# One layer of a hybrid encoder trunk: x is transposed before its norm, and the reciprocal rms goes onto the projections' results

## Chip, cores and metric

The kernel runs on one core of a Trainium2 chip. The metric is the device time of one execution in microseconds (us); lower is better. Engines: PE (TensorE), DVE (VectorE), ACT (ScalarE), POOL (GpSimd), SP (SyncE, which only issues transfers here).

## What is computed

One layer on 512 tokens of width 1024, batch 1. The part of the reference that the change touches:

```python
h = rms_norm(x, norm_mix_gain[l])      # x * rsqrt(mean(x*x) + eps) * gain
proj = h @ w_in[l]                     # 1024 x 3328, split into head groups
sb_q, sb_k, sb_v, hg_q, hg_f, hg_i, hg_g, mem_q = jnp.split(proj, split_points, axis=-1)
```

The head groups then go into stick-breaking attention (8 heads), a gated linear recurrence (4 heads) and attention into 256 memory tokens (4 heads). Their results are concatenated, multiplied by `w_out` and added to x. A retrieval over 16384 single-neuron experts follows (queries, top-k over product keys, gated sum of the chosen experts) and is added too. The rms of a token is one number for its row of h, so it may be applied to x before the product or to the row of `proj` after it.

## The kernel before

Tokens lie in four blocks of 128 (`xs[0..3]`). Every fp32 matmul operand is split in two: a rounded high part (`hhi`, `whi`) and the rest (`hlo`, `wlo`). A product is three matmuls, high by high, high by low, low by high (`mm3`, L413). Each matmul wants the contracted dimension on the partitions, so h is needed transposed: `hhi` and `hlo` hold k = 0..7 slices of 128 features by 512 tokens.

`x_norm` (L564) is the opening. It takes the squares' sums of the four blocks (ACT for blocks 0 and 2, DVE for 1 and 3), gets the reciprocal rms for two blocks at a time (`rsqrt`, L344: logarithm and exponential on ACT, one correction step on DVE), scales x by it into `hn`, and transposes: for each k one PSUM bank `nt` gets four 128x128 transposes, one per block; ACT evicts it times the gain into `hhi`, DVE evicts it again minus `hhi` into `hlo`.

`WStream` (L371) brings the weights: pieces of 128x1024 fp32, two to a chunk of 256 columns. `split` (L388) rounds a piece into `whi` (on DVE for piece 0, on ACT for the others) and subtracts for `wlo` (on POOL for pieces 0 and 1, on DVE later).

`in_proj` (L594) calls `x_norm` and then goes through the chunks. For the recurrence's f and q and the attention's q and k it uses `proj_f` (L479: 24 matmuls of 512 tokens for half a chunk; the result has features on partitions and tokens along the free dimension). For the values, the gates and the memory queries it uses `proj_t` (L489: tokens on partitions, 256 features). ACT evicts most results, with a sigmoid or a plain copy; `forget_bound` (L441) makes the constants `lb`, `omlb` (its scratch tile is `gmx`).

The order of the work is not written out by hand. `Threads` (L209) runs generators (`in_proj`, the recurrence `hgrn`, `sbreak`, `memattn`, `outproj`, `query`, `topk`, `gather`, `dense` and others), and `Pace` (L116) keeps modelled clocks for each engine; the generator that could go on first by that model emits its next step. The emitted instructions run in that order on each engine's in-order queue. A step whose modelled cost or engine changes can so move the steps of others. Transfers are issued on SP's queue; in this program each issue from the ninth on waits for the one eight places before it. Nearly all instructions bear L202, the helper that emits them, so the names of their tiles tell them apart.

Names in the rows: `nt` PSUM of transposes, `pf` and `pt` PSUM of `proj_f` and `proj_t`, `fkq` the recurrence's f, k, q, `hs` its scores, `hk`/`hkt` and `st`/`Sst` its transposed keys and state, `sz`, `se`, `sa`, `so` the attention's steps, `op` the output projection.

Of the kernel before, what the change touches and what calls it, by code (L numbers as in the profile page):

```python
# [7 lines left out]
F32 = mybir.dt.float32  # L8
# [6 lines left out]
AF = mybir.ActivationFunctionType  # L15
OP = mybir.AluOpType
# [4 lines left out]
P = 128  # L21
D = 1024
KD = 8
T = 512
NT = 4
# [237 lines left out]
def tile_trunk_layer(ctx: ExitStack, tc: tile.TileContext, x, mem, w_in, w_kv, w_out, w_query,  # L263
# [12 lines left out]
    def bank(name="pb", dt=F32, shape=None):  # L276
        uid[0] += 1
        b = ps.tile(shape or [P, 512], dt, name=f"{name}{uid[0]}", tag="bank", bufs=8)
        PSUMS.add(b.tensor.name)
        return b  # L280
# [8 lines left out]
    page = slot("a2", NPG)  # L289
# [5 lines left out]
    def tmp(shape, dt=F32, name="tmp", bufs=2):  # L295
        uid[0] += 1
        t = sb.tile(shape, dt, name=f"{name}{uid[0]}", tag=name, bufs=bufs)
        return t

    def t2(shape, dt=F32, name="t"):  # L300
        uid[0] += 1
        t = sb.tile(shape, dt, name=f"{name}{uid[0]}", tag="t2", bufs=NT2)
        return t
# [3 lines left out]
    def f(ap):  # L307
        return ap.bitcast(F32)
# [4 lines left out]
    gn = cst.tile([P, gains.shape[1]], F32, name="gn")  # L313
    for t in range(NT):
        SP.dma_start(xs[t], x[t * P:(t + 1) * P])
        if t == 0:
            SP.dma_start(gn, gains)
    g_mix, g_mem, g_ffn, g_out = gn[:, 0:8], gn[:, 8:16], gn[:, 16:24], gn[:, 24:32]
    g_mq, g_mk = gn[:, 32:33], gn[:, 33:34]
    gam = gn[:, 34:42]  # L320
# [50 lines left out]
    class WStream:  # L371
# [16 lines left out]
        def split(self, s):  # L388
            if s >= len(self.items) or s in self.half:
                return  # L390
            self.load(s)
            w = self.raw[s]
            h = wpage([P, 4, 256], F32R, name="whi")
            if s:
                A.activation(h, w, AF.Copy)
            else:
                V.tensor_copy(h, w)
            lw = wpage([P, 4, 256], F32R, name="wlo")
            self.items[s][1].tensor_tensor(lw, w, f(h), op=OP.subtract)
            self.half[s] = (h, lw)  # L400
# [12 lines left out]
    def mm3(o, lh, ll, rh, rl, first, last):  # L413
        PE.matmul(o, lh, rh, start=first, stop=False)
        PE.matmul(o, lh, rl, start=False, stop=False)
        PE.matmul(o, ll, rh, start=False, stop=last)
# [57 lines left out]
    def hsl(lst, k, a, b):  # L474
        g = KD // len(lst)
        return lst[k // g][:, k % g, a:b]


    def proj_f(W, half):  # L479
        hi, lo = W  # L480
        b = bank("pf")
        for k in range(KD):
            cs = slice(half * P, half * P + P)
            mm3(b, hi[k // 4][:, k % 4, cs], lo[k // 4][:, k % 4, cs], hsl(hhi, k, 0, T), hsl(hlo, k, 0, T),
                k == 0, k == KD - 1)
        return b


# [55 lines left out]
    def mem_keys(memk):  # L544
# [16 lines left out]
        A.activation(memkT.rearrange("p a b -> p (a b)"), b, AF.Copy, scale=g_mk)  # L561
        th.set("memk")

    def x_norm():  # L564
        ss = tmp([P, 4], name="ss")
        rs = tmp([P, 4], name="rs")
        hn = [page([P, D], name="hn") for _ in range(NT)]
        def squares(p):
            A.activation(hn[p], xs[p], AF.Square, accum_out=ss[:, p:p + 1])
            V.tensor_tensor_reduce(hn[p + 1], xs[p + 1], xs[p + 1], 1.0, 0.0, OP.mult, OP.add, ss[:, p + 1:p + 2])  # L570

        squares(0)
        rsqrt(rs[:, 0:2], ss[:, 0:2], D, 2)
        squares(2)
        A.activation(hn[0], xs[0], AF.Copy, scale=rs[:, 0:1])
        steps = rsqrt_(rs[:, 2:4], ss[:, 2:4], D, 2)
        next(steps)
        V.tensor_scalar(hn[1], xs[1], rs[:, 1:2], None, op0=OP.mult)
        for _ in steps:
            pass  # L580
        A.activation(hn[2], xs[2], AF.Copy, scale=rs[:, 2:3])
        V.tensor_scalar(hn[3], xs[3], rs[:, 3:4], None, op0=OP.mult)
        ws.split(0)
        for k in range(KD):
            if k == 1:
                ws.split(1)
            b = bank("nt")
            for t in range(NT):
                PE.transpose(b[:, t * P:(t + 1) * P], hn[t][:, k * P:(k + 1) * P], ident)
            A.activation(hhi[k // 2][:, k % 2], b, AF.Copy, scale=g_mix[:, k:k + 1])  # L590
            V.scalar_tensor_tensor(hlo[k // 2][:, k % 2], b, g_mix[:, k:k + 1], f(hhi[k // 2])[:, k % 2],
                                   op0=OP.mult, op1=OP.subtract)

    def in_proj():  # L594
        x_norm()
        yield
        forget_bound()
        th.add(consts(), at=pace.unit)
        th.add(mem_norm(), at=pace.unit)
        for _ in range(2):  # L600
            fkq = big3([P, 3, 2, T], name="fkq")
            for i, lst in enumerate((fh, Kh, Qh)):
                lst.append(fkq[:, i])
        big["hv"] = hv = page([P, NT, 256], name="hv")
        big["hg"] = hg = page([P, NT, 256], name="hg")
        for _ in range(2):
            hsc.append(page([P, NT, 2, P], name="hsc"))
        big["ho"] = page([P, NT, 256], name="ho")
        for c in range(2):
            W = ws.get()  # L610
            for hf in range(2):
                b = proj_f(W, hf)
                h = 2 * c + hf
                fo = fh[c][:, hf]
                A.activation(fo, b, AF.Sigmoid)
                V.tensor_scalar(fo, fo, omlb[:, h:h + 1], lb[:, h:h + 1], op0=OP.mult, op1=OP.add)
                V.tensor_scalar(Kh[c][:, hf], fo, -1.0, 1.0, op0=OP.mult, op1=OP.add)
                yield "pe"
        for c in range(2):
            W = ws.get()  # L620
            for hf in range(2):
                b = proj_f(W, hf)
                A.activation(Qh[c][:, hf], b, AF.Sigmoid)
                V.tensor_tensor(Qh[c][:, hf], Qh[c][:, hf], b, op=OP.mult)
                yield "pe"
        for c in range(2):
            W = ws.get()
            for t in range(NT):
                if t % 2 == 0:
                    b = bank("pt")  # L630
                o = b[:, (t % 2) * 256:(t % 2) * 256 + 256]
                proj_t(W, t, o, hhi, hlo)
                if t % 2:
                    bb = b.rearrange("p (t n) -> p t n", t=2)
                    if c == 0:
                        A.activation(hv[:, t - 1:t + 1], bb, AF.Copy)
                    else:
                        A.activation(hg[:, t - 1:t + 1], bb, AF.Sigmoid)
                        V.tensor_tensor(hg[:, t - 1:t + 1], hg[:, t - 1:t + 1], bb, op=OP.mult)
                yield "pe"  # L640
            th.set("hg_in")
        yield from mem_proj()
        for lst, nm in ((sq, "sq"), (sk, "sk")):
            for _ in range(2):
                lst.append(page([P, 2, T], name=nm))
        for _ in range(2):
            sv.append(page([P, NT, 256], name="sv"))
        big["mq"] = mq = page([P, NT, 256], name="mq")
        for c in range(2):
            W = ws.get()  # L650
            for hf in range(2):
                b = proj_f(W, hf)
                A.activation(sq[c][:, hf], b, AF.Copy, scale=0.125)
                yield "pe"
        for c in range(2):
            W = ws.get()
            for hf in range(2):
                b = proj_f(W, hf)
                A.activation(sk[c][:, hf], b, AF.Copy)
                yield "pe"  # L660
        th.set("sb_z")
        for c in range(2):
            W = ws.get()
            for t in range(NT):
                if t % 2 == 0:
                    b = bank("pt")
                proj_t(W, t, b[:, (t % 2) * 256:(t % 2) * 256 + 256], hhi, hlo)
                if t % 2:
                    A.activation(sv[c][:, t - 1:t + 1], b.rearrange("p (t n) -> p t n", t=2), AF.Copy)
                yield "pe"  # L670
        th.set("sb_in")
        W = ws.get()
        for t in range(NT):
            if t % 2 == 0:
                b = bank("pt")
            proj_t(W, t, b[:, (t % 2) * 256:(t % 2) * 256 + 256], hhi, hlo)
            if t % 2:
                A.activation(mq[:, t - 1:t + 1], b.rearrange("p (t n) -> p t n", t=2), AF.Copy)
            yield "pe"
        th.set("mem_in")  # L680
        yield "pe"
# [830 lines left out]
    def gather():  # L1512
        yield f"tk{GT}"
        e, gate = gat["e"], tk[GT][:, 2]
        act = tmp([P, 128], name="act", bufs=1)
        wgt = tmp([P, 128], name="wgt", bufs=1)

        done = [0]

# [109 lines left out]
```

## Time and profile before

| | before |
|---|---|
| median of 3 runs | 1596.6 us (1595.94 to 1597.5) |
| the profiled execution: time, and span from first to last instruction | 1597.62 us, 1595.9 us |
| PE busy | 1557.3 us (98%) |
| DVE, ACT, POOL busy | 1265.1 (79%), 756.1 (47%), 353.0 (22%) |
| chain that ended last, by engine | PE 92%, DVE 5%, ACT 2%, issue 1% |
| mean granted TensorE clock | 0.993 |

Busy time counts a matmul until its modelled end, so matmuls overlap and a busy PE need not be at its peak. The chain that ended last is followed back from the last instruction to what released each one; it says where time was spent in a row, not what the engines did beside it. All times below are in us from the span's start.

### The profile page before, as it was taken

How to read it: one execution, taken by the hardware profiler on the slowest of the kernel's cores; microseconds unless marked ns; L12 is line 12 of the kernel's file. 1: busy time of each engine (PE TensorE's matmuls, PEld its weight loads, DVE VectorE, ACT ScalarE, POOL GpSimd, SP SyncE). 2: the span in 40 equal slices, each digit the busy share in tenths (PEclk: the TensorE clock that was granted, in tenths of full speed). 3: DMA queues.
4: the chain of work that ended last, by engine and by line, in shares of the span. 5: the costliest groups of instructions: out<-in, count | busy, mean ns of one | idle time of the engine just before them, and what ended most of it. 6: DMA issues, size and time to landing. Idle time of an engine off the chain costs nothing.

```text
span 1595.9 us, 25702 instructions
## 1 busy us (share of the span) xinstructions
PE 1557.3 (98%) x9359; PEld 1427.8 (89%) x9359; DVE 1265.1 (79%) x2531; ACT 756.1 (47%) x1431; POOL 353.0 (22%) x340
## 2 busy tenths in 40 slices
PE   6999998998999999999999999999999999999998
PEld 5898998898999999999999999988888888888887
DVE  5465568789877898788878978759888888888886
ACT  5422267764344455675656755434333333333332
POOL 3000000000442211122111210234333333333320
PEclk9999999999999999999999999999999999999999
DMA  6232102274687777989888988999999999999991
GB/s 251 80 106 80 53 28 90 92 237 151 211 325 255 258 234 278 306 270 329 268 279 276 303 267 275 323 392 408 408 405 379 380 363 369 384 380 371 351 369 64
DMA packets 164527, 424.81 MB, mean 266 GB/s; under 512 B 13616, under 2 KB 62768, under 8 KB 164400
## 3 DMA queue, kind: packets, MB, share of 16 engines
q1 hardware_dynamic: 68400, 238.60, 40.9%
q0 software_dynamic: 36864, 134.23, 23.0%
q10 hardware_dynamic: 59136, 50.34, 9.8%
q8 instruction: 73, 1.20, 0.3%
q14 instruction: 54, 0.44, 0.1%
HBM read 368.60 MB, written 54.53 MB: 265 GB/s over the span
## 4 chain that ended last, share of the span: by engine, by line
PE 92%; DVE 5%; ACT 2%; issue 1%; DMA 0%; SPq 0%; ACTq 0%; DVEq 0%
PE ua L202 33%; PE pin L202 33%; PE pf L202 5%; PE pt L202 4%; PE qf L202 4%; PE gb L202 3%; PE op L202 2%; PE hs L202 2%; PE qp L202 1%; PE sz L202 1%; DVE wlo L202 1%; ACT se L202 1%; PE qs L202 1%; PE so L202 1%; DVE tka L202 1%
## 5 line engine op out<-in xcount | busy, mean ns | idle before, releaser
L202 DVE TENSOR_TENSOR xlo<-ex,xhi 128x1024 fp32r<-128x1024 f32 x256 | 312.7, 1222 | 105.0 <-issue 49.2
L202 POOL DMA_INDIRECT row<-in_u_rows_dram,eidx x128 | 163.3, 1276 | 896.3 <-DVE tka L202 401.3
L202 PE MATMUL ua<-h2hi,xhi 128*128 128x384 f32 x1024 | 348.9, 341 | 0.0
L202 PE MATMUL ua<-h2hi,xlo 128*128 128x384 f32 x1024 | 342.9, 335 | 0.0
L202 PE MATMUL ua<-h2lo,xhi 128*128 128x384 f32 x1024 | 342.5, 335 | 0.0
L202 ACT ACTIVATE whi<-w 128x384 fp32r<-128x384 f32 (+1 forms) x205 | 144.9, 724 | 343.1 <-DVE w L202 323.7
L202 PE MATMUL pin<-xhi,whi 128*128 128x512 f32 x768 | 298.9, 389 | 1.5 <-ACT whi L202 1.5
L202 PE MATMUL pin<-xlo,whi 128*128 128x512 f32 x768 | 298.9, 389 | 1.2 <-DVE xlo L202 1.2
L202 PE MATMUL pin<-xhi,wlo 128*128 128x512 f32 x768 | 298.8, 389 | 0.0
L202 ACT ACTIVATE xhi<-ex 128x1024 fp32r<-128x1024 f32 x256 | 268.7, 1051 | 25.3 <-issue 9.1
L202 DVE TENSOR_TENSOR wlo<-w,whi 128x384 fp32r<-128x384 f32 (+1 forms) x204 | 161.2, 805 | 115.2 <-PE pin L202 61.3
L202 POOL DMA_INDIRECT row<-in_v_rows_dram,eidx x128 | 172.6, 1349 | 289.2 <-DVE w L202 214.0
L202 PEld LDWEIGHTS ua<-h2lo,xhi 128*128 128x128 f32 x1024 | 192.5, 188 | 0.0
L202 PEld LDWEIGHTS ua<-h2hi,xhi 128*128 128x128 f32 x1024 | 192.2, 188 | 0.1
L202 PEld LDWEIGHTS ua<-h2hi,xlo 128*128 128x128 f32 x1024 | 192.2, 188 | 0.0
L202 PEld LDWEIGHTS pin<-xhi,whi 128*128 128x128 f32 x768 | 144.2, 188 | 31.8 <-ACT whi L202 1.9
L202 PEld LDWEIGHTS pin<-xlo,whi 128*128 128x128 f32 x768 | 144.2, 188 | 31.3 <-DVE xlo L202 1.5
L202 PEld LDWEIGHTS pin<-xhi,wlo 128*128 128x128 f32 x768 | 144.2, 188 | 29.8
L202 DVE SCALAR_TENSOR_TENSOR xg<-row,wgt,xg 128x1024 f32<-128x1024 f32 x128 | 163.8, 1280 | 0.6
L202 DVE CUSTOM_DVE_ANT_0 row<-row,xr 128x1024 f32<-128x1024 f32 x128 | 155.4, 1218 | 4.1 <-DMA row<-in_u_rows_dram,eidx 4.1
L202 ACT ACTIVATE gel<-ua 128x384 f32<-128x384 f32 x128 | 62.8, 491 | 191.3 <-PE ua L202 188.0
L202 ACT ACTIVATE oh<-oh,gpg 128x128 f16<-128x128 f16 x256 | 84.4, 436 | 16.3 <-DVE oh L202 4.0
(255 smaller groups left out, 2292.4 us busy)
## 6 DMA issues: line engine op xcount, KB each, us to landing
ex<-in_u_t_dram SPq DMA_DIRECT2D x128, 512.0 KB
ex<-in_v_rows_dram SPq DMA_DIRECT2D x128, 512.0 KB
gel<-gel ACTq DMA_DIRECT2D x64, 384.0 KB
gd<-stg ACTq DMA_DIRECT2D x48, 512.0 KB
G<-gd SPq DMA_DIRECT2D x48, 512.0 KB
gel<-gel SPq DMA_DIRECT2D x64, 384.0 KB
w<-in_w_query_dram SPq DMA_DIRECT2D x32, 512.0 KB
w<-in_w_in_dram SPq DMA_DIRECT2D x26, 512.0 KB
```

The lines of the kernel that those rows point to most:

```text
L202: r = fn(*args, **kw)
```

## The change

x is transposed as it is, block by block in the order in which the blocks arrive, into all eight PSUM banks (`x_split`); the eviction multiplies only by the gain. The sums of squares are taken beside this, and the reciprocal rms of all four blocks comes at the end as `rs4` (tokens on partitions). `x_norm` now runs after the first two halves of the first weight chunk: it multiplies the identity by `rs4` into `dg`, and four matmuls with a matrix of minus ones spread it over all partitions, as `rsb` (128x512). Results of `proj_f` are multiplied by `rsb` on DVE when they are evicted; results of `proj_t` get `rs4` as ACT's scale, one token block at a time. The first `proj_f` takes its low-weight matmuls late (`rests`: after the fourth and after the eighth k). `whi` of piece 0 moves from DVE to ACT, `gains` are loaded after the four blocks of x, and the two scratch tiles of `gather` now lie in `rsb`.

```diff
     for t in range(NT):
         SP.dma_start(xs[t], x[t * P:(t + 1) * P])
-        if t == 0:
-            SP.dma_start(gn, gains)
+    SP.dma_start(gn, gains)
...
-            if s:
-                A.activation(h, w, AF.Copy)
-            else:
-                V.tensor_copy(h, w)
+            A.activation(h, w, AF.Copy)
...
-    def proj_f(W, half):
+    def proj_f(W, half, rests=None):
...
+            PE.matmul(b, hi[k // 4][:, k % 4, cs], hsl(hhi, k, 0, T), start=k == 0, stop=False)
+            PE.matmul(b, hi[k // 4][:, k % 4, cs], hsl(hlo, k, 0, T), start=False, stop=False)
+            for j in range(dict(rests or {}).get(k, k if rests is None else KD), k + 1):
+                PE.matmul(b, lo[j // 4][:, j % 4, cs], hsl(hhi, j, 0, T), start=False, stop=j == KD - 1)
...
+    def x_split():
+
+        ss = tmp([P, 4], name="ss")
+        junk = [page([P, D], name="hn") for _ in range(2)]
+        bs = [bank("nt") for _ in range(KD)]
...
+        for t in range(NT):
+            for k in range(KD):
+                PE.transpose(bs[k][:, t * P:(t + 1) * P], xs[t][:, k * P:(k + 1) * P], ident)
+        for p in (0, 2):
+            A.activation(junk[0], xs[p], AF.Square, accum_out=ss[:, p:p + 1])
+        V.tensor_tensor_reduce(junk[1], xs[1], xs[1], 1.0, 0.0, OP.mult, OP.add, ss[:, 1:2])
+        for k in range(KD):
+            A.activation(hhi[k // 2][:, k % 2], bs[k], AF.Copy, scale=g_mix[:, k:k + 1])
+            if k in (0, 3):
+                ws.split(k // 3)
+            V.scalar_tensor_tensor(hlo[k // 2][:, k % 2], bs[k], g_mix[:, k:k + 1], f(hhi[k // 2])[:, k % 2],
+                                   op0=OP.mult, op1=OP.subtract)
+        A.activation(junk[0], xs[3], AF.Square, accum_out=ss[:, 3:4])
+        rsqrt(rs4, ss, D, 4)
+
     def x_norm():
...
+        dg = t2([P, 4, P], name="dg")
+        V.tensor_tensor(dg, ident[:, None, :].to_broadcast([P, 4, P]), rs4[:, :, None].to_broadcast([P, 4, P]), op=OP.mult)
+        b = bank("nt")
+        for t in range(NT):
+            PE.matmul(b[:, t * P:(t + 1) * P], f(nones), dg[:, t], start=True, stop=True)
+        A.activation(rsb, b, AF.Copy, scale=-1.0)
...
+            if c == 0:
+                bs = [proj_f(W, 0, rests=((3, 0), (7, 4))), proj_f(W, 1)]
+                x_norm()
             for hf in range(2):
-                b = proj_f(W, hf)
+                b = proj_f(W, hf) if c else bs[hf]
...
-                A.activation(fo, b, AF.Sigmoid)
+                V.tensor_tensor(fo, b, rsb, op=OP.mult)
+                A.activation(fo, fo, AF.Sigmoid)
...
-                A.activation(sq[c][:, hf], b, AF.Copy, scale=0.125)
+                V.scalar_tensor_tensor(sq[c][:, hf], b, 0.125, rsb, op0=OP.mult, op1=OP.mult)
...
-                A.activation(sk[c][:, hf], b, AF.Copy)
+                V.tensor_tensor(sk[c][:, hf], b, rsb, op=OP.mult)
...
-                    A.activation(sv[c][:, t - 1:t + 1], b.rearrange("p (t n) -> p t n", t=2), AF.Copy)
+                    for i in (t - 1, t):
+                        A.activation(sv[c][:, i], b[:, (i % 2) * 256:(i % 2) * 256 + 256], AF.Copy, scale=rs4[:, i:i + 1])
```

`hg_q` is changed as f is (into a tile `zq`), and `hv`, `hg` and `mq` as `sv` is.

How instructions move, at three places. First ACT, in the opening; before, from its first square on:

```order
L202 ACTIVATE hn_126,ss_124<-x_66 128x1024
L199 ACT_TABLE_LOAD
L202 ACTIVATE rr_134<-rv_132 128x2
L202 ACTIVATE rr_134<-rr_134 128x2
L202 ACTIVATE hn_128,ss_124<-x_68 128x1024
L202 ACTIVATE hn_126<-x_66,rs_125 128x1024
L202 ACTIVATE rr_149<-rv_146 128x2
L202 ACTIVATE rr_149<-rr_149 128x2
L202 ACTIVATE hn_128<-x_68,rs_125 128x1024
L202 ACTIVATE hhi_95<-nt_163,gn 128x512
L202 ACTIVATE whi_170<-w_105 128x1024
L202 ACTIVATE hhi_95<-nt_174,gn 128x512
```

With the change:

```order
L202 ACTIVATE hn_127,ss_126<-x_66 128x1024
L202 ACTIVATE hn_127,ss_126<-x_68 128x1024
L202 ACTIVATE hhi_95<-nt_129,gn 128x512
L202 ACTIVATE whi_174<-w_103 128x1024
L202 ACTIVATE hhi_95<-nt_130,gn 128x512
L202 ACTIVATE hhi_96<-nt_131,gn 128x512
L202 ACTIVATE hhi_96<-nt_132,gn 128x512
L202 ACTIVATE whi_184<-w_105 128x1024
L202 ACTIVATE hhi_97<-nt_133,gn 128x512
L202 ACTIVATE hhi_97<-nt_134,gn 128x512
L202 ACTIVATE hhi_98<-nt_135,gn 128x512
L202 ACTIVATE hhi_98<-nt_136,gn 128x512
```

The reciprocal roots (`rr`) and the scalings (`hn` from `rs`) no longer stand ahead of the first eviction (`hhi`); the first weight copy (`whi` of `w_103`) now stands between the first and the second.

Second DVE, between the reciprocal rms (`rs`) and the first eviction of a projection, with the change:

```order
L202 TENSOR_TENSOR rs_119<-rr_200,rq_203 128x4
L202 TENSOR_TENSOR gmx_208<-gn 128x4
L202 TENSOR_TENSOR gmx_208<-gn,gmx_208 128x4 x2
L202 TENSOR_TENSOR gmx_208<-gmx_208 128x4
L202 RECIPROCAL gmx_208<-gmx_208 128x4
L202 TENSOR_TENSOR lbt<-gmx_208 128x4
L202 TENSOR_SCALAR lbt<-lbt 128x4
L202 TENSOR_TENSOR wlo_226<-w_107,whi_224 128x1024
L202 TENSOR_TENSOR wlo_230<-w_109,whi_228 128x1024
L202 TENSOR_TENSOR dg_290<-ident,rs_119 128x512
L202 TENSOR_TENSOR fkq_217<-pf_240,rsb 128x512
L202 TENSOR_SCALAR fkq_217<-fkq_217,lbt 128x512
```

The product with the identity (`dg`) stands behind the forget bound (`gmx`, `lbt`) and behind the split of the second chunk (two `wlo`). Before, the eviction of the first projection was on ACT and there was no `dg`.

Third DVE, at the end of the projections, where the recurrence's last score steps (`hsc` from `hs`) and first key copies (`hkt`) stand; before:

```order
L202 COPY hkt_1755<-hk_1752 128x256
L202 COPY_PREDICATED hsc_237<-mk_314,hs_1722 128x512
L202 TENSOR_TENSOR fkq_233<-fkq_233 128x8x64 x2
L202 TENSOR_TENSOR fkq_233<-fkq_233 128x8
L202 COPY hkt_1817<-hk_1814 128x256
L202 TENSOR_TENSOR wlo_1822<-w_1380,whi_1820 128x1024
L202 TENSOR_TENSOR wlo_1826<-w_1382,whi_1824 128x1024
L202 COPY Sst_119<-st_1867 128x64 x2
L202 COPY hkt_1915<-hk_1912 128x256
L202 SCALAR_TENSOR_TENSOR se_1898<-sz_1514,se_1898 128x128
```

With the change:

```order
L202 COPY_PREDICATED hsc_222<-mk_333,hs_1776 128x512
L202 COPY hkt_1820<-hk_1817 128x256
L202 TENSOR_TENSOR wlo_1824<-w_1382,whi_1822 128x1024
L202 TENSOR_TENSOR wlo_1828<-w_1384,whi_1826 128x1024
L202 COPY_PREDICATED hsc_222<-mk_333,hs_1812 128x512
L202 TENSOR_TENSOR fkq_218<-fkq_218 128x8x64 x2
L202 TENSOR_TENSOR fkq_218<-fkq_218 128x8
L202 COPY hkt_1918<-hk_1915 128x256
L202 SCALAR_TENSOR_TENSOR se_1902<-sz_1505,se_1902 128x128
```

Before, the first state copy (`Sst`) and a third key copy stand ahead of the attention step (`se`); with the change only two key copies do, and the last score steps stand between them. In PE's order the last score matmuls (`hs`) stand behind 792 of the 960 matmuls of `pf` and `pt` before, and behind 864 with the change. From the queries of token block 0 on, the order on every engine is that of before.

## Rows read from the trace of the kernel before

**Rows 1.** Waits of TensorE, whole run: who waits, for whom; us in total, times, longest.
```profile
PE nt L202 <- ACT hn L202: 12.8, 2, 11.4
```

**Rows 2.** Busy us by stretch: PE, PEld, DVE, ACT, POOL (records); granted clock, DMA share, GB/s.
```profile
140.00:180.00 40.00, 40.00 (x274) 36.35 (x273) 23.95 (x44) 9.99 (x20) 0.00 (x0) 1.00 0.19 65
...
335.00:350.00 15.00, 13.64 (x111) 12.88 (x111) 14.51 (x43) 11.43 (x24) 0.00 (x0) 1.00 0.67 230
```

**Rows 3.** Chain that ended last, opening: start us, us, what.
```profile
14.06 5.61 PE nt L202 x30
```

**Rows 4.** Timeline, PE: start us, us, instruction [idle before <- releaser].
```profile
19.43 0.48 PE L202 MATMUL pf<-hhi,whi 128*128 128x512 f32 x1
...
30.45 0.39 PE L202 MATMUL pf<-hhi,whi 128*128 128x512 f32 x1
```

**Rows 5.** Timeline, SyncE's DMA issues in the opening.
```profile
7.30 0.33 SPq L202 DMA_DIRECT2D mem<-in_mem_dram  x1
...
8.72 0.33 SPq L202 DMA_DIRECT2D w<-in_w_in_dram  x1
...
9.96 0.33 SPq L202 DMA_DIRECT2D w<-in_w_in_dram  x1
...
11.24 0.33 SPq L202 DMA_DIRECT2D w<-in_w_in_dram  x1
```

**Rows 6.** Timeline of the opening: ACT, DVE and POOL.
```profile
4.33 1.06 ACT L202 ACTIVATE hn<-x 128x1024 f32<-128x1024 f32 x1 [2.24 <-DMA x<-in_x_dram]
...
5.30 0.19 ACT L202 ACTIVATION_READ_ACCUMULATOR hn<-x 128x1 f32 x1
...
8.65 0.17 DVE L202 TENSOR_SCALAR rv<-ss 128x2 f32<-128x2 f32 x1
...
9.93 0.16 DVE L202 TENSOR_TENSOR rs<-rr,rq 128x2 f32<-128x2 f32 x1
...
14.30 4.69 POOL L202 TENSOR_TENSOR wlo<-w,whi 128x1024 fp32r<-128x1024 f32 x2 [13.16 <-DVE whi L202]
...
14.79 0.69 ACT L202 ACTIVATE hhi<-nt,gn 128x512 fp32r<-128x512 f32 x1 [0.78 <-PE nt L202]
...
16.32 4.36 ACT L202 ACTIVATE hhi<-nt,gn 128x512 fp32r<-128x512 f32 x7
...
17.03 4.71 DVE L202 SCALAR_TENSOR_TENSOR hlo<-nt,gn,hhi 128x512 fp32r<-128x512 f32 x7 [0.77 <-ACT hhi L202]
...
21.65 0.15 DVE L202 TENSOR_TENSOR gmx<-gn 128x4 f32<-128x4 f32 x1
...
22.24 1.99 ACT L202 ACTIVATE whi<-w 128x1024 fp32r<-128x1024 f32 x2
...
23.32 2.40 DVE L202 TENSOR_TENSOR wlo<-w,whi 128x1024 fp32r<-128x1024 f32 x2 [0.17 <-ACT whi L202]
```

**Rows 7.** Transposes: timeline of PE at 15 and 63 us; busy by stretch, as rows 2.
```profile
14.97 1.27 PE L202 MATMUL nt<-ident,hn 128*128 128x128 f32 x5
...
63.09 1.03 PE L202 MATMUL nt<-ident,hn 128*128 128x128 f32 x8
...
16.00:17.00 1.00, 1.00 (x7) 1.00 (x6) 0.26 (x1) 1.00 (x3) 1.00 (x2) 1.00 1.07 418
```

**Rows 8.** Chain that ended last, 60 to 420 us: start us, us, what.
```profile
79.38 1.78 PE hs L202 x16
```

**Rows 9.** Groups, 20 to 215 us: x count | busy us, mean ns | idle before.
```profile
L202 DVE TENSOR_TENSOR fkq<-fkq,pf 128x512 f32<-128x512 f32 x4 | 2.7, 687 | 10.4 <-ACT fkq L202 10.4
...
L202 ACT ACTIVATE sq<-pf 128x512 f32<-128x512 f32 x4 | 2.4, 597 | 19.3 <-PE pf L202 19.3
```

**Rows 10.** Timeline, DVE, end of the projections.
```profile
202.77 0.36 DVE L202 COPY Sst<-st 128x64 f32<-128x64 f32 x2 [0.70 <-PE st L202]
```

**Rows 11.** Busy us by stretch, attention and output stage; columns as rows 2.
```profile
275.00:277.50 2.50, 2.50 (x13) 2.50 (x13) 2.46 (x5) 1.06 (x1) 0.00 (x0) 0.50 0.48 152
...
340.00:342.50 2.50, 2.50 (x23) 2.50 (x23) 2.47 (x10) 1.81 (x2) 0.00 (x0) 1.00 0.84 251
```

More of the change, by code (lines that the diff above doesn't have):

```diff
@@ L476, in hsl @@
         return lst[k // g][:, k % g, a:b]
-    def proj_f(W, half):
+    def proj_f(W, half, rests=None):
         hi, lo = W
         b = bank("pf")
+        cs = slice(half * P, half * P + P)
         for k in range(KD):
-            cs = slice(half * P, half * P + P)
-            mm3(b, hi[k // 4][:, k % 4, cs], lo[k // 4][:, k % 4, cs], hsl(hhi, k, 0, T), hsl(hlo, k, 0, T),
-                k == 0, k == KD - 1)
+            PE.matmul(b, hi[k // 4][:, k % 4, cs], hsl(hhi, k, 0, T), start=k == 0, stop=False)
+            PE.matmul(b, hi[k // 4][:, k % 4, cs], hsl(hlo, k, 0, T), start=False, stop=False)
+            for j in range(dict(rests or {}).get(k, k if rests is None else KD), k + 1):
+                PE.matmul(b, lo[j // 4][:, j % 4, cs], hsl(hhi, j, 0, T), start=False, stop=j == KD - 1)
         return b
@@ L562, in mem_keys @@
         th.set("memk")
-    def x_norm():
[L565 to L592, printed above, removed]
@@ new lines, in tile_trunk_layer @@
+    rs4 = cst.tile([P, 4], F32, name="rs4")
+    rsb = cst.tile([P, T], F32, name="rsb")
+    def x_split():
+        ss = tmp([P, 4], name="ss")
+        junk = [page([P, D], name="hn") for _ in range(2)]
+        bs = [bank("nt") for _ in range(KD)]
+        A.eng.preload_act_table_set(ACT_SETS[AF.Ln])
+        A.table = ACT_SETS[AF.Ln]
+        for t in range(NT):
[12 more added lines that the diff above has]
+        rsqrt(rs4, ss, D, 4)
@@ L594, in in_proj @@
+    def x_norm():
+        dg = t2([P, 4, P], name="dg")
[4 more added lines that the diff above has]
+        A.activation(rsb, b, AF.Copy, scale=-1.0)
     def in_proj():
-        x_norm()
+        x_split()
         yield
@@ L622, in in_proj @@
                 b = proj_f(W, hf)
-                A.activation(Qh[c][:, hf], b, AF.Sigmoid)
-                V.tensor_tensor(Qh[c][:, hf], Qh[c][:, hf], b, op=OP.mult)
+                z = t2([P, T], name="zq")
+                V.tensor_tensor(z, b, rsb, op=OP.mult)
+                A.activation(Qh[c][:, hf], z, AF.Sigmoid)
+                V.tensor_tensor(Qh[c][:, hf], Qh[c][:, hf], z, op=OP.mult)
                 yield "pe"
@@ L634, in in_proj @@
                     bb = b.rearrange("p (t n) -> p t n", t=2)
[L635 to L639, printed above, removed]
+                    for i in range(2):
+                        r = rs4[:, t - 1 + i:t + i]
+                        if c == 0:
+                            A.activation(hv[:, t - 1 + i], bb[:, i], AF.Copy, scale=r)
+                        else:
+                            A.activation(hg[:, t - 1 + i], bb[:, i], AF.Sigmoid, scale=r)
+                            V.scalar_tensor_tensor(hg[:, t - 1 + i], bb[:, i], r, hg[:, t - 1 + i], op0=OP.mult, op1=OP.mult)
                 yield "pe"
@@ L677, in in_proj @@
             if t % 2:
-                A.activation(mq[:, t - 1:t + 1], b.rearrange("p (t n) -> p t n", t=2), AF.Copy)
+                for i in (t - 1, t):
+                    A.activation(mq[:, i], b[:, (i % 2) * 256:(i % 2) * 256 + 256], AF.Copy, scale=rs4[:, i:i + 1])
             yield "pe"
@@ L1514, in gather @@
         e, gate = gat["e"], tk[GT][:, 2]
-        act = tmp([P, 128], name="act", bufs=1)
-        wgt = tmp([P, 128], name="wgt", bufs=1)
+        act, wgt = rsb[:, 0:P], rsb[:, P:2 * P]
         done = [0]
```

## Prediction

> **What bounds the kernel now.** I began with the waits of TensorE over the whole run, since PE is busy for 98% of the span: the reader is to see that one wait stands apart, the transposes `nt` on the normalised rows `hn`, 12.8 us in all, 11.4 of it ahead of the very first [rows 1]. Then the busy time by stretch: between 140 and 180 us PE is busy for all of 40.00 us while DVE has 23.95 and ACT 9.99; between 335 and 350 us DVE is busy for 14.51 of 15.00 and PE has gaps [rows 2]. So the program has a serial opening, then projections that PE alone bounds, then a mixed stage (about 215 to 420 us) in which the releaser alternates, then the dense stage, bound by PE again. Third, the chain of waits for the opening: the transposes start at 14.06 and take 5.61 us for 30 [rows 3]. The first projection matmul starts at 19.43; the 49th, which opens the second weight chunk, at 30.45, so 0.2296 us each [rows 4]. Whatever the change wins must appear as an earlier third projection, and then has to survive the mixed stage.
>
> **When x can be used.** In this program each of SyncE's issues from the ninth on waits for the transfer eight places before it, so the issue times show what had landed by then: x1 at 7.30, x2 at 8.72, x3 at 9.96, the first weight piece at 11.24 us [rows 5]; ACT saw x0 at 4.33 [rows 6]. Moving `gains` behind x3 leaves the bytes ahead of the first weight piece as they were, so I keep 11.24 for that, x1 to x3 are at latest where they were, and `gains` lands between 9.96 and 11.24; I take 10.4.
>
> **The new opening, step by step.** Removed: the norm ahead of the transposes (two reciprocal roots, four scalings). The 32 transposes stay but run by row block as it lands. In the opening of before they are slow: five take 1.27 us, where eight of the same shape take 1.03 us at 63 us [rows 7]; the granted clock of that stretch reads 1.00 all the same [rows 7]. I take 0.21 us, between 5.61/30 [rows 3] and 1.27/5. x0's eight then run from 4.33 to 6.0, x1's from 7.30 to 9.0, x2's to 10.7, and bank 0 is complete with the first of x3's, at 10.9 to 11.1; with x a little sooner, at 10.2. So the first `hhi` starts at 10.8 (bounds 10.2 and 11.5).
>
> From there ACT sets the pace: eight `hhi` with one weight copy among them took from 14.79 to 20.68, which is 5.89 us [rows 6]. The first weight copy now runs on ACT too, 1.0 us more (two take 1.99) [rows 6], so the last `hhi` ends at 10.8 + 6.9 = 17.7. If `hhi` starts at 10.2 the first weight copy waits for 11.24 and the end is the same within 0.2, so the lower bound gives little. The last `hlo` ended 1.06 us after the last `hhi` (21.74 against 20.68) [rows 6]: 18.8. POOL needs 4.69 us for its two `wlo` [rows 6], starting when each weight copy is done, at 12.5 and about 15.3: done by 14.9 and 17.7. That is early enough, because the first projection now asks for `wlo` only after its fourth and eighth k. After the last `hlo` five matmuls remain, 1.15 us: the first projection ends at 19.9. In before that was 19.43 + 24 x 0.2296 = 24.94, so the gain here is 5.0 us. The second projection follows without a wait, 5.5 us, to 25.4.
>
> Added on PE: four matmuls that spread `rs4` over the partitions. The nearest row is `hs`, of the same type and shape: 16 records for eight program matmuls in 1.78 us [rows 8], so four cost 0.89. Do they wait? Square of x3 and its read, 1.16 us from 4.33 to 5.49 for x0 [rows 6], end at 18.9, then the reciprocal root, 1.44 us from `rv` at 8.65 to the end of `rs` at 10.09 [rows 6]: 20.3. The forget bound, two weight copies and two `wlo` stand ahead of `dg` on DVE; from the first `gmx` at 21.65 to the end of the two `wlo` was 4.07 us [rows 6], so DVE is free at 24.4 and `dg`, 0.7 us, ends at 25.1. PE arrives at 25.4. It is covered by 0.3 us only; without that cover it costs up to 0.7. The third projection starts at 26.3 instead of 30.45: **4.2 us** gained (3.2 if `hhi` starts at 11.5 and `dg` is late; 4.6 at best).
>
> **The rest of the projections.** Evictions that multiply by `rsb` move to DVE. There are 16 new or moved multiplies of 128x512 out of PSUM; the row with the same operands is 687 ns [rows 9], so 11.0 us, and 0.7 for `dg`. ACT gives up eight evictions of 597 ns [rows 9], 4.8 us, and gets ten others cut into halves. DVE was busy for 60% of the stretch shown and PE for all of it [rows 2], so I cost these edits at nothing; the cover is DVE's idle time. Should it fail, each late pair of `wlo` stalls PE (the rival below). The planner also lets the recurrence slip: the last score matmuls move behind 864 of 960 projection matmuls where they stood behind 792, and one `Sst` pair and one `hkt` copy move past the last projection. That pair cost 0.36 us [rows 10] and the copy about as much, 0.78 in all, in a stage where DVE is often the releaser. I charge half, 0.4; the ends are 0 (hidden) and 4.2 (all of the gain gone in a new order of short steps). From the last third of the mixed stage on all engines have the order of before, so nothing is added after it; the last third and the dense stage just start earlier.
>
> Sum: -4.2 + 0.4 = -3.8 us against the profiled execution's 1597.6 (span 1595.9). That execution was 1.0 above the median of the runs, 1596.6; against the median the forecast is **1592.8 us**. A measurement of this kernel tells 0.2% from no change, 3.2 us: below 1593.4 is faster, above 1599.8 slower.
>
> **Rivals.**
> *The mixed stage eats the gain* (25%). There PE waits for short ACT and DVE steps, and the order has changed by a few rows on each engine between about 200 and 310 us. For it: DVE 97% busy at 335 to 350 us [rows 2]. Against: DVE had slack in the 70 us before, so no backlog enters the stage. If 2 to 5 us of new waits appear, the time is 1594.5 to 1597.5.
>
> *The projections start at half clock* (8%). In the mixed stage after a wait the granted clock was 0.50, the lower level of 1.2 GHz, and 13 matmuls fitted where 23 of the same shape do at 1.00 [rows 11]. In the changed opening transposes come in bursts with gaps, and the first projection is fed piece by piece. At 23/13 of the price the first projection takes 9.7 us from 12.4, to 22.1 instead of 19.9: 1595.0. Against it: before, the transposes themselves sped up while they ran without a gap. The Trainium skill ("TensorE: Matmul & The Clock Gate", What's actually happening) says that the throttled state is the default and that activity releases it; the slow first transposes agree [rows 7], though the recorded clock does not show them. If bursts with gaps do not release it, that rule makes this rival the outcome.
>
> *x is not what bounds the opening* (6%). If `gains` lands after the first weight piece, the evictions start at 12 and the change does not do what it says: gain 3.0, 1594.0.
>
> *DVE becomes the bound of the projections* (slower, 8%). On DVE's queue each multiply out of PSUM waits for a projection to end with the next weights' `wlo` behind it. In before the pair ended at 25.72 and was wanted at 30.45, a lead of 4.7 us [rows 4, 6]. From the point at which the multiplies, the recurrence and the mem branch delay a pair by more than that, PE waits at each of the remaining chunks; half of a `wlo` pair, 1.2 us, on six of 14 chunks is 7 us: 1600.
>
> **How the numbers follow.** The forecast as worked out has 53%; of its own spread (-2.5 to -6) about nine tenths lie beyond -3.2, with the order also able to turn out better. The rivals hold the rest, and all but one stay within 0.2% or just at it. Faster 0.48, same 0.43, slower 0.09. The range 1589.5 to 1597.5 takes in the best opening with a lucky mixed stage and the first three rivals. The forecast's own range is 1590.5 to 1594.
>
> **What would show it.** Right: first transposes on x near 4.4 us; first `hhi` near 10.8; the first projection's last matmul near 19.9, with gaps inside it; four `nt` matmuls on `dg` without a wait ahead of them; the third projection at 26.3; no waits of PE up to 210 us, and in the mixed stage about the waits of before. Wrong: a wait of PE on `wlo` or `dg`; first projection matmuls 0.4 us apart; or a third projection at 26 and a dense stage that starts where it did, which would put the loss in the mixed stage.

## The result, and the profile after

The changed kernel takes **1601.7 us** (median of 15 runs) where the kernel before took 1595.72 beside it: ratio 1.0054, 95% interval 1.0039 to 1.0068. It is slower by half a per cent; 1592.8 was forecast, the range ended at 1597.5. Its runs lie in two groups, nine from 1597.0 to 1602.4 and six from 1609.0 to 1613.4, where the kernel before has 1594.6 to 1597.5; the profiled execution (1611.3) is of the upper group.

First the opening. The page's head, then TensorE's waits, then the timeline, all of the changed kernel:

```profile
span 1609.6 us, 25736 instructions
...
PE 1579.2 (98%) x9367; PEld 1432.8 (89%) x9367; DVE 1272.7 (79%) x2540; ACT 754.5 (47%) x1432; POOL 356.3 (22%) x340
...
PEclk9999999998999999999999999999999999999999
```

```profile
PE xt L202 <- ACT sq L202: 5.9, 3, 3.3
PE nt L202 <- DMA x<-in_x_dram: 4.6, 1, 4.6
...
PE pf L202 <- ACT whi L202: 0.8, 1, 0.8
```

```profile
4.62 6.44 PE L202 MATMUL nt<-ident,x 128*128 128x128 f32 x32 [4.62 <-DMA x<-in_x_dram]
...
10.22 0.69 ACT L202 ACTIVATE hhi<-nt,gn 128x512 fp32r<-128x512 f32 x1 [1.06 <-PE nt L202]
...
11.90 0.50 PE L202 MATMUL pf<-hhi,whi 128*128 128x512 f32 x1 [0.85 <-ACT whi L202]
...
19.20 0.39 PE L202 MATMUL pf<-hhi,whi 128*128 128x512 f32 x1
...
23.35 0.72 DVE L202 TENSOR_TENSOR dg<-ident,rs 128x512 f32<-128x512 f32 x1
...
24.80 1.05 PE L202 MATMUL nt<-dg,nones 128*128 128x128 f32 x8
25.60 0.48 PE L202 MATMUL pf<-hhi,whi 128*128 128x512 f32 x1
```

The wait of 12.8 us on the normalised rows [rows 1] is gone, 4.6 on x is left (the row on `xt` belongs to a later stage and stood at 5.8 before). The second projection starts at 19.20, `dg` is ready before PE asks for it, and the third projection starts at 25.60 instead of 30.45 [rows 4]. The opening did what was forecast, and a little more.

Then the chain of waits. The expert stages (the generator `dense`) have two products: `ua`, tokens times the experts' input rows, 384 columns a matmul, and `pin`, gated results times the experts' output rows, 512 columns. Their longest unbroken pieces (start, length, matmuls), before and after:

```profile
479.87 74.89 PE ua L202 x432
...
1068.28 521.65 PE pin L202 x2300
```

```profile
475.64 74.89 PE ua L202 x432
...
1066.71 536.93 PE pin L202 x2300
```

From these rows the 13.7 us between the two profiled spans (1595.9 and 1609.6; the medians are 6.0 apart) add up: third projection -4.85; from there to the first `ua` 449.42 before and 450.04 after, +0.62; from the first `ua` to the first `pin` 588.41 and 591.07, +2.66; the 2300 `pin` matmuls **+15.28**; together 13.71. The `pin` row is one piece: TensorE waits for nobody in it, before or after. Its matmuls simply follow each other at 0.2334 us where it was 0.2268. The groups by operation say the same (busy us, mean ns; a matmul here lasts to its modelled end and overlaps the next), before and then after:

```profile
L202 PE MATMUL ua<-h2hi,xhi 128*128 128x384 f32 x1024 | 348.9, 341 | 0.0
L202 PE MATMUL pin<-xhi,whi 128*128 128x512 f32 x768 | 298.9, 389 | 1.5 <-ACT whi L202 1.5
...
L202 PE MATMUL pt<-whi,hhi 128*128 128x256 f32 x160 | 46.5, 290 | 0.0
```

```profile
L202 PE MATMUL ua<-h2hi,xhi 128*128 128x384 f32 x1024 | 351.0, 343 | 0.0
...
L202 PE MATMUL pin<-xhi,whi 128*128 128x512 f32 x768 | 305.3, 397 | 1.5 <-ACT whi L202 1.5
...
L202 PE MATMUL pt<-whi,hhi 128*128 128x256 f32 x160 | 45.9, 287 | 0.0
```

512 columns became slower, 384 a little, and 256 faster. And by stretch (columns as in [rows 2]), with the granted clock at 1.00 in both, before and after; the number in brackets behind PE counts its matmuls:

```profile
1080.00:1580.00 500.00, 500.00 (x2207) 414.16 (x2206) 434.20 (x527) 181.87 (x248) 180.16 (x134) 1.00 0.94 363
```

```profile
140.00:180.00 40.00, 40.00 (x282) 36.47 (x281) 23.65 (x42) 10.78 (x22) 0.00 (x0) 1.00 0.18 62
...
1080.00:1580.00 500.00, 500.00 (x2145) 404.99 (x2144) 421.68 (x512) 177.16 (x241) 181.91 (x133) 1.00 0.95 361
```

In a stage of which no instruction was changed, 62 matmuls fewer fit into 500 us. Below, "pitch" is the distance of two matmuls' starts within such a row. So the question for the chip was what sets the pitch. Each kernel has one trace; pitches below are of that one execution.

### The profile page after: what moved, and what is told of

It is laid out like the page before. It is cut to its first block, busy times and chain, and to the rows that moved or that the text cites. A ratio compares the mean times of both kernels' runs of the same rounds, so it can differ in the third digit from the quotient of the medians.

```text
span 1609.6 us, 25736 instructions
## 1 busy us (share of the span) xinstructions
PE 1579.2 (98%) x9367; PEld 1432.8 (89%) x9367; DVE 1272.7 (79%) x2540; ACT 754.5 (47%) x1432; POOL 356.3 (22%) x340
## 4 chain that ended last, share of the span: by engine, by line
PE 94%; DVE 3%; ACT 1%; issue 0%; DMA 0%; ACTq 0%; DVEq 0%
PE pin L202 33%; PE ua L202 33%; PE pf L202 6%; PE pt L202 4%; PE qf L202 4%; PE gb L202 3%; PE op L202 2%; PE sz L202 2%; PE hs L202 2%; PE qp L202 1%; PE so L202 1%; PE qs L202 1%; DVE wlo L202 1%; DVE tka L202 1%; PE nt L202 1%; PE mo L202 0%
## 5 line engine op out<-in xcount | busy, mean ns | idle before, releaser
L202 PE MATMUL pin<-xhi,whi 128*128 128x512 f32 x768 | 305.3, 397 | 1.5 <-ACT whi L202 1.5
L202 PE MATMUL pin<-xlo,whi 128*128 128x512 f32 x768 | 305.3, 397 | 1.2 <-DVE xlo L202 1.2
L202 PE MATMUL pin<-xhi,wlo 128*128 128x512 f32 x768 | 305.2, 397 | 0.0
L202 DVE SCALAR_TENSOR_TENSOR xg<-row,rsb,xg 128x1024 f32<-128x1024 f32 x128 | 163.8, 1280 | 0.6
```

What stands on the lines that cost most here:

```text
L202: r = fn(*args, **kw)
```

## Experiments

### All tiles moved together

The change adds two tiles ahead of all large ones, `rs4` and `rsb`, 2080 bytes of each partition. Theory A: the places of the operands set the pitch. Rival B: the order or the new operations do. C: it is the chip that a run got. Four kernels, each with one unused tile (and the scratch of `gather` put into it where it is large enough):

```diff
     lbt = cst.tile([P, 8], F32, name="lbt")
+    pad = cst.tile([P, 8], F32, name="pad")   # 520 and 512 in the second and third kernel
```

> The kernel before with one unused 32-byte tile ahead of the larger tiles, so that x, hhi, hlo, the weights and their halves start 32 bytes later (at a multiple of 64 bytes, as in the changed kernel) and nothing else differs. Theory A, the pitch of a 512-column matmul hangs on where its operands lie: the pin matmuls of the long stretch go from 0.2268 to about 0.233 us each and the time rises to 1600-1613 us. Theory B, the loss comes from the order or the new operations of the change: 0.2268 us each and 1595.7 us within 0.2%. Theory C, it hangs on the chip the run got: both kernels move alike.

Measured: 1595.35 us, ratio 0.9999 (0.999 to 1.0008); `pin` 2300 in 521.65.

> The kernel before with a tile of 2080 bytes where the changed kernel puts rs4 and rsb, and the gather's two scratch tiles inside it as the changed kernel has them: every large tile lies at the changed kernel's address, and no operation of the change is made. Theory A (addresses): 0.233 us per pin matmul, 4 to 15 us over the kernel before, about the changed kernel's 1601.7 plus the 4 us that its opening gains, so 1600-1615. Theory B (order, new operations): 1595.7 us, 0.2268 us per pin matmul.

Measured: 1595.68, ratio 1.0001 (0.9992 to 1.001); `pin` 2300 in 523.27.

> The kernel before with a tile of 2048 bytes (the gather's scratch in it): all large tiles move by 2048 bytes and keep their 32 bytes past a multiple of 64. Theory A in its form by 64 bytes: no change, 1595.7 us and 0.2268 us per pin matmul. Theory A in a form by a larger step (a 4096-byte tile now crosses another boundary): 4 to 15 us slower. Theory B: no change.

Measured: 1596.2, ratio 1.0005 (0.9996 to 1.0014); 523.25.

> The changed kernel with one unused 32-byte tile ahead of the larger tiles, so that they lie 32 bytes past a multiple of 64 as in the kernel before. Theory A by 64 bytes: 0.2268 us per pin matmul again and 1590.5 to 1592.5 us, faster than the kernel before by the 3 to 5 us of the opening. Theory B (order, new operations): 1601.7 us as the changed kernel, 0.233 us. A form by a larger step: between, since the 2048 bytes of rsb remain.

Measured: 1601.73, ratio 1.0042 (1.0023 to 1.0061); the pitch stayed at 0.233. Each kernel kept its own pitch, and theory A seemed to have fallen; C fell with it, since the kernel before took 1595.33 on the same chip. The lengths of 521.65 and 523.25 differ by some 3 us at the lower granted clock at the start of `pin`, not by the pitch of the rest; by stretch, second kernel:

```profile
1066.50:1068.00 1.50, 1.50 (x5) 1.20 (x4) 1.17 (x2) 0.30 (x1) 0.00 (x0) 0.50 1.03 410
```

### Parts of the change

> The changed kernel with the first projection in the plain order (three matmuls per piece of x, no weight rests put off). The address theory has fallen: four runs with moved addresses kept each kernel's own pitch, and the pitch is there from the first projection on, for the whole execution. Theory D, the pitch is set in the first 20 us by how TensorE starts (transposes that trickle in as x lands, a rest, matmuls that wait): 512-column matmuls at 0.233 us still, 1598-1613 us. Theory D2, it is the put-off rests alone: 0.2267 us and 1591-1593 us. Theory E, it is the later operations (scaling by rsb): 0.233 us, 1598-1613.

```diff
-                bs = [proj_f(W, 0, rests=((3, 0), (7, 4))), proj_f(W, 1)]
+                bs = [proj_f(W, 0), proj_f(W, 1)]
```

Measured: 1606.94 us, ratio 1.0069 (1.0043 to 1.0094). From the first to the 25th projection matmul it takes 9.19 us, with the put-off rests 7.30, so these bring 1.9 us. Part of that is the clock, which the changed kernel has at 1.00 there: without the put-off rests TensorE waited 1.7 us for `whi`, ran two matmuls and waited 1.7 us for `wlo`; then the granted clock was 0.50, the level of 1.2 GHz, and matmuls started 0.427 us apart:

```profile
14.30:17.70 3.40, 3.35 (x8) 2.67 (x9) 2.79 (x5) 3.40 (x7) 2.96 (x4) 0.50 1.02 411
```

What makes up the rest of the 5.2 us between this median and the changed kernel's is not shown. The pitch does not come from the rests, but this trace shows a second one: 0.2333 in the projections and 0.2289 in `pin`. By the chain and by stretch:

```profile
1068.03 528.34 PE pin L202 x2300
```

```profile
1080.00:1580.00 500.00, 500.00 (x2186) 410.22 (x2186) 428.83 (x519) 180.25 (x245) 179.37 (x134) 1.00 0.95 363
```

> The changed kernel with its 32 transposes ordered by piece instead of by token tile, each piece beginning with the last tile of x: TensorE now starts when all of x is there and runs its transposes without a wait. Theory D (how TensorE starts): the pitch goes back to 0.2267 us in most executions; the opening loses about 4 us, so 1594-1597 us. Theory E (later operations): 0.233 us and 1602-1615 us.

```diff
-        for t in range(NT):
-            for k in range(KD):
+        for k in range(KD):
+            for t in reversed(range(NT)):
                 PE.transpose(bs[k][:, t * P:(t + 1) * P], xs[t][:, k * P:(k + 1) * P], ident)
```

Measured: 1602.99 us, ratio 1.0052 (1.0033 to 1.0071), 2145 matmuls from 1080 to 1580 us: theory D falls.

> The kernel before with 32 more transposes, of x as it lands, into banks that nobody reads: TensorE starts as in the changed kernel, with the same trickle and then a rest, and all else is the kernel before. Theory D: 512-column matmuls at 0.233 us, 1600-1613 us. Theory E: 0.2267 us and 1595.7 us (or 1593-1595 if the warm clock helps the real transposes by half of their 3 us).

```diff
+        bs = [bank("nt") for _ in range(KD)]
+        for t in range(NT):
+            for k in range(KD):
+                PE.transpose(bs[k][:, t * P:(t + 1) * P], xs[t][:, k * P:(k + 1) * P], ident)
         def squares(p):
```

Measured: 1595.07 us, ratio 0.9998 (0.9988 to 1.0008), pitch 0.2267: D falls from this side too.

> The opening of the kernel before, but the changed kernel's consumers: every projection's result is multiplied by rsb and rs4, which hold ones. Theory E (the later operations): 0.233 us, 1602-1615 us. Theory D: 0.2267 us and 1595-1597 us (the opening gains nothing, the scaling costs 0.4).

The body of `x_split` is that of the old `x_norm`, weight copies and `gains` are as before, the first projection has no put-off rests, and of the new `x_norm` this is left:

```diff
     def x_norm():
-        dg = t2([P, 4, P], name="dg")
...
+        V.memset(rs4, 1.0)
+        V.memset(rsb, 1.0)
```

Measured: 1604.71 us, ratio 1.0072 (1.0047 to 1.0096). The time spoke for E, the trace against it: the pitch was 0.2267. What it lost lies mostly in the mixed stage (the first `ua` starts at 485.70, before at 479.87). There TensorE waits for `oo`, a result of DVE, for 6.4 us at once, where it was 0.4:

```profile
PE xt L202 <- DVE oo L202: 6.4, 1, 6.4
```

In the chain, the last unbroken row of the output projection is longer than before by 62 matmuls. First this kernel, then before:

```profile
358.18 31.68 PE op L202 x264
```

```profile
360.11 24.50 PE op L202 x202
```

Why the planner's order left them there was not tried.

### Tiles moved against each other

By now four traces had the slow pitch and six the other, and the list of where each kernel's tiles lie (the addresses in the built programs) told them apart. The first four runs had moved all tiles together. But the change also moves some tiles against others: `rs`, `rv`, `rr` and `rq` (960 bytes) get their places at first use, and in the changed opening that is after the first weights are split, so the eight pages for the weight halves (`whi`, `wlo`, later `xhi`, `xlo`) slip ahead of them. Places in bytes past a multiple of 256:

```
                               weight-half pages   hhi, hlo, h2hi   w's halves in pin
before, b_early                       96                 96               96
b_pad32, b_as_after, b_scaled        128                128              128
b_pad2048                             96                 96               96
after, a_norests, a_dense            192                128              128
a_pad32                              224                160              160
```

> The changed kernel with the small scratch tiles rs, rv, rr and rq given their room ahead of the eight pages for the weight halves (whi, wlo, xhi, xlo), as the kernel before has them; the change leaves them to be placed behind, which moves these pages 960 bytes against all other tiles (from 128 to 192 past a multiple of 256 bytes). No instruction and no order changes. All slow-pitch traces so far (4 kernels) have the pages there, all 6 traces at 0.2267 us don't. Theory A2, the place of the pages for the weight halves: 0.2267 us per pin matmul, 1590 to 1593 us, a spread of some 3 us and faster than the kernel before. Theory E (the later operations): 0.233 us, 1598 to 1613 us as the changed kernel.

```diff
         ss = tmp([P, 4], name="ss")
+        tmp([P, 4], name="rs")
+        for n, k in (("rv", 5), ("rr", 5), ("rq", 4)):
+            tmp([P, 12], name=n, bufs=k)
         junk = [page([P, D], name="hn") for _ in range(2)]
```

Measured: **1590.8 us** (1587.0 to 1592.2), ratio **0.9968** (0.9957 to 0.9979). The chain, and two stretches:

```profile
470.16 74.89 PE ua L202 x432
...
1058.47 523.19 PE pin L202 x2300
```

```profile
140.00:180.00 40.00, 40.00 (x288) 37.08 (x287) 24.16 (x42) 10.78 (x22) 0.00 (x0) 1.00 0.18 60
...
1080.00:1580.00 500.00, 500.00 (x2208) 414.20 (x2207) 427.66 (x515) 177.55 (x242) 174.08 (x130) 1.00 0.92 355
```

> The kernel before with the same 2080 and 960 bytes moved the other way: x, its halves, the raw weights and the eight pages for the weight halves lie at the very addresses of the changed kernel; no instruction changes but the gather's scratch, which lies in the added tile. Theory A2 (place of the pages): 0.229 to 0.2334 us per pin matmul, 1600 to 1616 us, with the changed kernel's wide spread. Theory E: 0.2267 us and 1595.5 us with a spread of 3.

```diff
     lbt = cst.tile([P, 8], F32, name="lbt")
+    pad = cst.tile([P, 520], F32, name="pad")
...
         ss = tmp([P, 4], name="ss")
+        for _ in range(8):
+            wpage([P, 4, 256], F32R, name="wz")
         rs = tmp([P, 4], name="rs")
```

Measured: 1611.62 us, ratio 1.009 (1.0072 to 1.0108), with none of the change's operations:

```profile
1069.39 538.48 PE pin L202 x2300
```

It differs from `b_as_after` (1595.7) in where the pages lie against the other tiles, and so does `a_fix` from the changed kernel; every engine's instructions are the same in each pair, only addresses differ. So 960 bytes of scratch, placed ahead of the pages or behind them, are worth 16 us in the kernel before (1611.6 against 1595.7) and 11 in the changed one (1601.7 against 1590.8); the change itself is a gain. What remained was the rule, and this kernel of matmuls alone was made for it:

```diff
+    def segment(sa, sm, n=24, cols=512):
+        b = bank("pb")
+        for q in range(n):
+            w = wt[:, sa // 4 + 128 * (q % 4):sa // 4 + 128 * (q % 4) + 128]
+            m = mv[:, sm // 4 + 512 * (q % 2):sm // 4 + 512 * (q % 2) + cols]
+            PE.matmul(b[:, 0:cols], w, m, start=q == 0, stop=q == n - 1)
```

> A kernel of matmuls alone; it leaves out the whole computation of the reference and writes a constant. 24 matmuls of 512 columns for each of 16 places of the stationary 128x128 operand (0 to 480 past a multiple of 512 bytes in steps of 32) and 8 places of the moving one (0 to 224), through and back, then 384 and 256 columns at fewer places. Theory A2 in its plain form, the place of the stationary operand by itself: 0.2267 us with it at 96 and 128, 0.229 to 0.2334 at 192 and 224, whatever the moving operand. A2 in its relative form: 0.2267 on the diagonal where both lie alike by 128, more off it. If only the load of the full kernel (other engines at the memory) makes the pitch: 0.2267 us everywhere.

Its timeline, 15 matmuls in a row each, from the first start to the last one's modelled end (some 0.39 us behind its start):

```profile
387.33 3.56 PE L202 MATMUL pb<-mv,wt 128*128 128x512 f32 x15
...
398.40 3.67 PE L202 MATMUL pb<-mv,wt 128*128 128x512 f32 x15
...
86.62 3.60 PE L202 MATMUL pb<-mv,wt 128*128 128x512 f32 x15
...
1351.11 3.66 PE L202 MATMUL pb<-mv,wt 128*128 128x512 f32 x15
```

The first has both operands at 128, the second the stationary one at 192 and the moving one at 128. The last two are the same pair of places (448 and 0), on the way through and back, with two pitches. From the starts of the last twelve of each segment, pitch in ns by place of the stationary operand less that of the moving one, modulo 256 (a range where pairs differ):

```
difference        0      32      64         96     128    160     192           224
512 columns   226.7   233.3   233.3      234.2   233.3  233.3   228.9 (233.3)  233.3
384 columns   173.3   173.3   174.8      173.3   176.5  176.7   173.3          176.7
256 columns   120.0   118.2   113.3-117.8  117.1-120   118.3  120.0   117.8    117.8
```

For 512 columns that is 31 or 32 segments at each difference, over 16 places of the one operand and 8 of the other (at 128 three gave 231.7 to 232.8, and one segment of the 32 at 192 gave 233.3); for 384 and 256 columns it is four. So the relative form of A2 holds with a step of 256 bytes, not 128, and no other engine is needed for it. Read back: in the projections `pf` the weights are stationary, which makes 192 - 128 = 64 in the changed kernel; in `pin` the page is the moving operand, 128 - 192, which is 192 modulo 256, the one place with two pitches. In `pt`, too, it is 192, where 256 columns are faster than at 0. All three agree with the traces above.

> The changed kernel in its mended layout with 32 unused bytes ahead of the eight pages for the weight halves: they now lie 160 past a multiple of 256 bytes and everything else that TensorE reads 128, so stationary minus moving operand is 32 in the feature-major projections (pf) and the u stage (ua), and 224 in the last stage (pin) and the token-major projections (pt). By the table of the matmul-only kernel: pf 233.3 ns, pin 233.2 (both passes agreed there, so no second value and a spread of some 4 us), ua 173.3, pt 117.7. From the mended kernel's 1590.8 us: pin +2304 x 0.0066 = 15.2, the some 400 others of 512 columns +2.6, the 1304 of 256 columns -2.6, ua 0: 1606 us, 1603 to 1609. If only certain places are bad by themselves (192 and 224 past 256, theory A2 in its plain form): 1591 us.

```diff
             tmp([P, 12], name=n, bufs=k)
+        tmp([P, 8], name="pad", bufs=1)
```

Measured: 1604.06 us (1599.5 to 1607.0), ratio 1.0054 (1.0041 to 1.0067): 32 unused bytes cost 13 us. `pf` and `pin` ran at 233.3, `ua` at 173.5, `pt` at 116.7 ns, a little under the table's 117.8. The runs spread over 7.4 us where some 4 were expected; the table has only one pitch at 224, so two pitches do not explain this spread.

```profile
1058.18 536.91 PE pin L202 x2300
```

## Why the prediction was wrong

**The opening** was right in its mechanism and came out early: first `hhi` 10.22 (10.8 forecast), first projection done at 19.20 (19.9), third at 25.60 (26.3), so 4.85 us instead of 4.2. The matmuls on `dg` found it ready since 24.07, 0.7 us ahead; a cover of 0.3 was forecast.

**The rivals** did not come. The projections did not start at half clock: the transposes ran slowly again, 25 in 5.58 us, and then the first projection had pitches of 0.23 to 0.34 us (once 0.79), the longer ones while `hhi` and `hlo` were still being written, at a granted clock of 1.00. So in this trace the Trainium skill's rule ("TensorE: Matmul & The Clock Gate", What's actually happening), that activity releases a throttled default, bore on the transposes only. In `a_norests`, though, which waits longer at the same place, eight matmuls did run at 0.50, so the put-off rests may be what kept this rival away. The prediction also took the clock of the slow transposes to be recorded as 1.00. It is not recorded: the trace's first record of the clock starts at 18.45 us in the kernel before and at 10.27 in the changed one, within 0.1 us of where the transposes go from 0.213 to 0.109 us each, and the 1.00 that the view gives for 16 to 17 us [rows 7] is what it prints where there is no record. DVE did not become the bound: PE is busy for 40.00 of 40.00 us between 140 and 180, DVE for 23.65. `gains` held nothing up. The mixed stage did not eat the gain: third projection to first `ua` was +0.62 beside the 0.4 charged, though traces with the order of before differ by more (`ua` starts at 476.0 to 479.9 in four of them), so that term is not resolved. In the mended layout `ua` starts at 470.16.

**The step that failed** is "nothing is added after it; the last third and the dense stage just start earlier". It took an unchanged instruction to have an unchanged price. The missing term is the pitch, and from the table it can be worked out for the changed kernel: 2304 `pin` matmuls at 228.9 or 233.3 instead of 226.7, +5.1 or +15.2; 384 `pf` +2.5; 576 `pt` at 117.8 instead of 120.0, -1.3; the `ua` stage +2.7 as measured above (3072 times the table's 1.5 would be 4.6). That is 9.0 or 19.1. (The 384 matmuls of `op` and 336 of `qf`, which also run at new differences, come to -0.8 and +0.5 by the table and are left out.) On top of the mended kernel's 1590.8 it gives 1599.8 or 1609.9, which is where the two groups of runs lie. With the operands' places kept, the forecast's -3.8 was measured as -4.8, inside its own range of 1590.5 to 1594.

At a difference of 192, `pin` ran at 228.9 ns in one kernel's trace (`a_norests`) and at 233.3 in four (`after`, `a_pad32`, `a_dense`, `b_shift`). That this makes the two groups is worked out and not shown, since only one execution of a kernel leaves a trace. The granted clock does not part them: its mean is 0.992 to 0.997 in the runs of the lower group and 0.991 to 0.997 in the upper. The same two sums on the kernel before, 1604.6 and 1614.7, are about the ends of `b_shift`'s six runs (1604.7 to 1615.5), but two of these lie between, at 1607.5 and 1609.9.

## What to carry to other kernels

Where a change adds or drops a tile, or uses one earlier or later for the first time, compare where the operands of the longest matmul stages lie before and after; for matmuls like these (rounded fp32, 512 columns, a new stationary operand for each) keep the stationary and the moving operand alike modulo 256 bytes. When a result contradicts a sound forecast, count a stage that was not changed: 2145 instead of 2207 matmuls in the same 500 us, with PE busy for all of them, told at once that no wait was at fault. To test a layout, move tiles against each other, since moving all of them together showed nothing here.

## What was not expected of the hardware

The pitch of back-to-back matmuls of the same shape went from 226.7 to 234.2 ns by nothing but where their two operands lie against each other, with the other engines idle. The Trainium skill ("SBUF — State Buffer", Who interferes with whom) gives TensorE one read port for the moving operand and one for weight loads and calls them independent. These runs do not agree in so far as the pitch depends on both places together; which part of the chip makes it so is not shown. At 192 the pitch can be either of two, and stay for the whole of a 500 us stage.

The transposes' slow start is a matter of what ran before: in the kernel with 32 transposes of x ahead of them (`b_early`), the same 30 took 3.50 us in the chain instead of 5.61 [rows 3].

```profile
14.32 3.50 PE nt L202 x30
```

Most of these 2.1 us was lost again by the end of the run (ratio 0.9998). That trace's first record of the granted clock (1.00) starts at 13.46 us, in the pause between the 32 slow transposes and these.
